# A half-precision Strassen matmul with GELU: staging, order and look-ahead changed

## The chip, the cores and the metric

The kernel runs on one NeuronCore of a Trainium2 chip. PE (TensorE) multiplies, DVE (VectorE) adds and transposes, ACT (ScalarE) copies, squares and applies GELU, POOL (GpSimd) issues loads and fetches, SP (SyncE) issues stores. The metric is the device time of one execution in microseconds (us).

## The reference, cut to what matters

```python
def reference(a: np.ndarray, b: np.ndarray) -> np.ndarray:   # 4096 x 4096, float32
    x = np.matmul(a, b)
    return 0.5 * x * (1 + np.tanh(np.sqrt(2 / np.pi) * (x + 0.044715 * x**3)))
```

## The kernel before, in words

**Tiling.** A, B and the output are cut into quadrants (11, 12, 21, 22) of 2048 x 2048. A block row `mb` (0 to 3) is 512 rows of each row half of A; a block column `nb` (0 to 3) is 512 columns of each column half of B. A group is a pair (mb, nb); there are 16, numbered 0 to 15, four to a block row. For each group the four output tiles of 512 x 512 are computed by Strassen's seven products M1 to M7 in float16: each product multiplies a sum or difference of A's quadrants (or one quadrant raw) by one of B's. The inner dimension of 2048 is handled in two chunks `c` of 1024, each in two quarters, so a product has four quarters `q`, and a quarter is 16 matmuls of 128 x 512: that is a step.

**Steps.** Everything is placed by a list of 504 steps, written as (group, product's place s, quarter q). Group 0 begins with 16 plain steps (chunk 0 without Strassen) and then has two steps for each product, numbers 16 to 29. Groups 1 to 9 have 28 steps each. In groups 10 to 15 the products M3 and M5, and in groups 13 to 15 also M2 and M1, are themselves split by Strassen into seven smaller products each, taken in the order of `PAIR`. `PRODUCTS` gives the order of products; a group before a change of block row uses `TURNING`, the last groups `FRESH`. The main loop at L1158 emits for each step: what stands in `before` for it (loads, transpositions, weighing), for the first six groups the operand sums of two steps later (`make_sums`), for later groups what the planner put into `tasks`, then `flush` and `combine` (pending output sums), and then the step's matmuls with `settle`, which takes finished sums from PSUM. [...]

**A.** A quadrant's part is loaded by POOL into a tile `stage` (two buffers, L192 and L221), as float16; DVE transposes it into `aT` (`turn_a`, L207); then ACT squares each row of the staged tile in place, with its sum (`weigh_row`, L267; `weigh_first` for the first block row, `weigh_rows` later), for a check of the magnitudes. Only then is the stage buffer free. In the first block row the text at L720 places loads (A.., B..), transpositions (T..) and weighing (W..) by step; names such as A22_1 give quadrant and chunk. Later block rows come in eight halves, in the order 11, 12, 22, 21; `TURNS` and `RAW_TURNS` give the step of each half's transposition as (s, q) counted from the group before the change, the load is placed `LOAD_AHEAD` steps before but not before the half two earlier is weighed, and the weighing takes the four steps after the transposition (L826 to L833).

**B.** Groups 0 to 5 load B raw into eight tiles `bR` whose places rotate between the quadrants when the block column changes (`b_slot`, L806 to L815): the next group's 12 takes the place of this group's 22. In the last of these groups for a block column, the operands of B that later groups will need are also stored to a scratch area in HBM: sums from `bS` by `make_sums` (L433) and raw quadrants by `keep_raw` (L402), both on SP's queue. `square` and `add_squares` (L300, L311) weigh B: ACT squares pieces, DVE adds them up; `TWO_GROUPS` places these for the block column that has two groups. Groups 6 to 15 fetch kept operands into tiles `bK` in the same eight places (`fetch`, L904), at most `FETCH_AHEAD` steps before use. `MAKES` lists when, in groups 6 to 10, operands for the later split products are made from kept ones by DVE (`make_split`, L997) and stored again (`k_split`); each entry is five sums in five consecutive steps.

**Sums of A.** From group 6 on the planner (L1104 to L1151) gives every operand sum of A a step: not earlier than a number of steps ahead of its use (`AHEAD` = 2, or `SPLIT_AHEAD` in split products), not before its buffer is free (three buffers `aS`, and in groups without makes three `bS` as well), and where an account of DVE's work per step leaves room (`sum_step`, L1041). Whole-block sums `aD` for the split products are planned by `plan_block` (L1075).

**Outputs.** `settle` (L621, for the last three groups `settle_fresh` at L665) copies PSUM tiles X and Y to `x7`, `x1` and `m5` tiles or combines them on DVE; `flush` and `emit` (L582, L608) apply GELU on ACT and store by SP. x7 has four buffers.

Of the kernel before, what the change touches and what calls it, by code (L numbers as in the profile page):

```python
# [16 lines left out]
P = 128  # L17
# [51 lines left out]
MAKES = (  # L69
    (6, 1, 0, 1, "M3"),  # L70
    (6, 2, 1, 1, "M5"),
    (6, 3, 2, 3, "M3"),
    (6, 4, 2, 3, "M5"),
    (7, 1, 3, 0, "M2"),
    (8, 2, 3, 2, "M3"),
    (8, 4, 0, 2, "M5"),
    (8, 5, 3, 2, "M1"),
    (9, 2, 0, 0, "M3"),
    (9, 2, 2, 0, "M5"),
    (9, 4, 2, 3, "M1"),  # L80
    (9, 5, 3, 3, "M2"),
    (10, 2, 2, 2, "M2"),
    (10, 4, 0, 0, "M1"),
)
STAY = ("M2", "M1")
STAY_AHEAD = 19
BLOCK_AHEAD = 12
SPLIT_AHEAD = 8
FETCH_AHEAD = 8
SPLITS = {M3_M5: (10, 11, 12, 13, 14, 15), M2_M1: (13, 14, 15)}  # L90
LOAD_AHEAD = 8

TURNS = ((2, 2), (3, 2), (4, 2), (5, 2), (6, 2), (7, 2), (9, 0), (10, 2))
RAW_TURNS = ((2, 2), (3, 2), (5, 2), (6, 1), (7, 1), (8, 1), (10, 1), (11, 1))

# [8 lines left out]

TWO_GROUPS = [x // 2 for x in range(16)] + [8 + 2 * x for x in range(16)]
N_WARM = 46
# [48 lines left out]
def half_path(  # L155
# [36 lines left out]
    def load_a(mb, quad, c, h=None):  # L192

        ih, kh = int(quad[0]) - 1, int(quad[1]) - 1
        n = NX if h is None else NX // 2
        x = 0 if h is None else h * n
        x0 = (ih * MH + mb * TM) // Q + x
        if not h:
            s = pool.tile([P, NX, RUN], F16, name="stage", tag="stage", bufs=2)
            staged[mb, quad, c] = s  # L200
        s = staged[mb, quad, c]
        return [
            (s[g * Q : (g + 1) * Q, x : x + n, :], a_v[kh, g, :, x0 : x0 + n, c * RUN : (c + 1) * RUN])
            for g in range(4)
        ]

    def turn_a(mb, quad, c, h=None):  # L207
# [5 lines left out]
        if mb:  # L213
            src = staged[mb, quad, h].rearrange("p x (c r) -> p c x r", c=CH)[:, c]
        else:
            src = staged[mb, quad, c][:, x, :]
        src = src.bitcast(U32).rearrange("p mb (jj q) -> p jj mb q", q=Q)
        dst = a_tiles[mb, quad, c].bitcast(U32).rearrange("p jj (mb q) -> p jj mb q", q=Q)
        nc.vector.transpose(dst[:, :, x, :], src)  # L219

# [65 lines left out]
    def weigh_first(quad, c, xs):  # L286

        ih, kh = int(quad[0]) - 1, int(quad[1]) - 1
        for x in xs:
            k = ((kh * CH + c) * 2 + ih) * NX + x  # L290
            weigh_row(stats["a"][:, k : k + 1], staged[0, quad, c][:, x, :])

# [372 lines left out]
    def settle_fresh(gi, name, i, X, Y):  # L665
# [6 lines left out]
        elif name == "M1":  # L672
            m1, x7 = keep("m5", X, 2), post["x7", i]
            tt(x7, x7, m1, ALU.add)
        elif name == "M4":
            emit(gi, i, 1, 0, new_y(), Y)
# [3 lines left out]
            waiting.append((gi, i, 0, 0, y, y))  # L680
        elif name == "M6":
            y = post.pop(("x1", i))
            tt(y, X, y, ALU.add)
            flush()
            waiting.append((gi, i, 1, 1, y, y))
# [34 lines left out]
    for n, whats in (  # L720
# [5 lines left out]
        (14, "T11_1 W11_1 A22_1 B11_1"),  # L726
        (16, "T12_1 W12_1:0-4"),
        (17, "W12_1:4-16 A21_1"),
        (18, "S2 S3 T22_1"),
        (23, "T21_1"),  # L730
        (34, "W22_1:0-1"),
        (35, "W22_1:1-2"),
        (36, "W22_1:2-3"),
        (37, "W22_1:3-4"),
        (38, "W22_1:4-5"),
        (39, "W22_1:5-6"),
        (40, "W22_1:6-7"),
        (41, "W22_1:7-8"),
        (42, "W22_1:8-9"),
        (43, "W22_1:9-10"),  # L740
        (44, "W22_1:10-11"),
        (45, "W22_1:11-12"),
        (46, "W22_1:12-13"),
        (47, "W22_1:13-14"),
        (48, "W22_1:14-15"),
        (49, "W22_1:15-16"),
        (50, "W21_1:0-1"),
# [73 lines left out]
    for gi in range(len(groups) - 1):  # L821
# [4 lines left out]
        for (quad, h), n in zip(halves, turns(gi)):  # L826
            at_step(max(n - LOAD_AHEAD, free_at.pop(0)), load, (load_half, (mb, quad, h)))
            free_at.append(n + 5)
            at_step(n, turn_half, mb, quad, h)
            for x in range(4):  # L830
                at_step(n + 1 + x, weigh_rows, mb, quad, h, list(range(NX // 2))[x * NX // 2 // 4 : (x + 1) * NX // 2 // 4])
            if h and quad in ("12", "21"):
                at_step(n + 5, weigh_half, mb, int(quad[0]) - 1)  # L833


    for nb, gi in last_raw.items():
        for s, (name, _, _, ob) in enumerate(PRODUCTS):
            for c in range(CH) if isinstance(ob, str) else ():
                at(gi, s, 2 * c, keep_raw, nb, name, ob, c)

# [263 lines left out]
    for gi in range(N_RAW, len(groups)):  # L1104
# [13 lines left out]
        for n in mine:  # L1118
# [14 lines left out]
            if not isinstance(o, str):  # L1133
                ahead = SPLIT_AHEAD if q in SPLIT else AHEAD
                only = any(n - ahead <= x <= n for x in makes) or makes and q not in SPLIT
# [17 lines left out]
    with tc.manual_schedule():  # L1153
# [4 lines left out]
        for n, step in enumerate(steps):  # L1158
            for fn, args in before.get(n, ()):
                fn(*args)  # L1160
            if n + AHEAD < len(steps):
                gi, s, q = steps[n + AHEAD]
                if s >= 0 and gi < N_RAW:
                    make_sums(gi, s, q)
# [9 lines left out]
            else:  # L1174
                multiply(*step)
            if step == (0, 2, QPH - 1):
                flush()
# [38 lines left out]
```

## Time and profile before

| what | us |
|---|---|
| median of 9 runs | 1571.2 |
| lowest and highest | 1567.64 and 1576.34 |
| profiled execution | 1575.39 |
| its span, first to last instruction | 1573.8 |
| PE busy | 1548.2 |
| DVE busy | 1139.0 |
| ACT busy | 601.3 |
| POOL busy (issuing) | 462.6 |
| end of the last matmul | 1567.5 |

The granted TensorE clock was 0.996 on average. In the lines shown below a timeline line has the start from the beginning of the span, the length, the engine, the line of the code, the operation, what it writes and reads, the shapes, the number of instructions merged, and in brackets the engine's idle time before it and what ended it. A line of the chain of waits has start, length and what was running. Line numbers are those of the kernel before.

### The profile page before, as it was taken

To read this page: it belongs to the slowest core of one execution; us is meant where nothing else is said; L and a number is where in the kernel's file an instruction comes from. 1 tells how busy PE (TensorE), PEld (TensorE's weight loads), DVE (VectorE), ACT (ScalarE), POOL (GpSimd) and SP (SyncE) were. 2 spreads that over 40 slices of the span, in tenths; PEclk is the share of its full clock that TensorE was granted. 3 is DMA by queue.
4 is the path that set the end of the run, shared out by engine and by line. 5 is a ranking of instruction groups with operands and counts; after the bars stand their busy time and mean duration, and the time that the engine had idled before them with its cause. 6 is when DMAs were issued, how large, how long until landed. Compare 5 with 4: busy or idle time off the path is not lost.

```text
span 1573.8 us, 22250 instructions
## 1 busy us (share of the span) xinstructions
PE 1548.2 (98%) x8110; PEld 794.5 (50%) x8110; DVE 1139.0 (72%) x1357; ACT 601.3 (38%) x1322; POOL 462.6 (29%) x830
## 2 busy tenths in 40 slices
PE   9999999999999999999999999999999999999998
PEld 4444444444444444444444444654746457677674
DVE  1597888889877887674656647978748677776774
ACT  5437456455543542111453211121345413232232
POOL 7763432441124311122231222221333312132130
PEclk9999999999999999999999999999999999999999
DMA  9999999994689988699997989897999959788693
GB/s 176 187 221 291 248 293 275 284 239 87 155 236 291 288 297 311 251 416 342 287 273 231 411 317 368 319 413 247 320 242 295 333 159 308 241 276 313 229 333 109
DMA packets 202789, 429.40 MB, mean 273 GB/s; under 512 B 20400, under 2 KB 102320, under 8 KB 200624
## 3 DMA queue, kind: packets, MB, share of 16 engines
q0 software_dynamic: 141472, 265.34, 65.5%
q1 hardware_dynamic: 61200, 162.56, 27.1%
q8 instruction: 66, 1.08, 0.3%
q14 instruction: 51, 0.42, 0.1%
HBM read 340.79 MB, written 162.53 MB: 320 GB/s over the span
## 4 chain that ended last, share of the span: by engine, by line
PE 74%; DMA 16%; DVE 4%; POOL 3%; issue 2%; ACT 1%; DVEq 0%; ACTq 0%; POOLq 0%
PE accX L466 35%; PE accY L466 26%; DMA stage<-in_a_dram 8%; PE accX L548 6%; PE accY L548 6%; DMA bR<-in_b_dram 4%; DMA k_split<-bS 2%; POOL bR L255 1%; POOL stage L255 1%; DMA k_M<-bS 1%; DVE aS L931 1%; DVE bS L428 1%; DVE x L619 1%; DVE bS L931 1%; DVE aT L219 0%
## 5 line engine op out<-in xcount | busy, mean ns | idle before, releaser
L466 PEld LDWEIGHTS <-aS 128*128 128x128 f16 x4192 | 410.1, 98 | 511.6 <-issue 13.8
L466 PE MATMUL accX<-bK,aS 128*128 128x512 f16 x1536 | 334.5, 379 | 2.4 <-DVE aS L931 2.1
L931 DVE TENSOR_TENSOR aS<-aT 128x2048 f16<-128x2048 f16 x182 | 216.6, 1217 | 90.6 <-PE accX L466 71.2
L466 PEld LDWEIGHTS <-aT 128*128 128x128 f16 x1600 | 156.6, 98 | 188.4 <-issue 0.4
L917 POOL DMA_DIRECT2D bK<-k_M x236 | 124.8, 533 | 398.2 <-PE accX L466 115.1
L255 POOL DMA_DIRECT2D bR<-in_b_dram x320 | 173.0, 543 | 213.1 <-DMA bR<-in_b_dram 105.4
L269 ACT ACTIVATE stage<-stage 128x512 f16<-128x512 f16 (+1 forms) x320 | 169.6, 532 | 140.3 <-DVE aT L219 101.4
L466 PE MATMUL accY<-bK,aS 128*128 128x512 f16 x896 | 195.0, 379 | 0.6 <-DVE aS L931 0.5
L610 ACT ACTIVATE x<-x 128x512 f32<-128x512 f32 x128 | 78.2, 628 | 251.5 <-DVE x L619 251.4
L466 PE MATMUL accX<-bS,aS 128*128 128x512 f16 x704 | 156.3, 383 | 6.9 <-DVE bS L428 4.3
L548 PEld LDWEIGHTS <-aS 128*128 128x128 f16 x1440 | 141.6, 98 | 26.4 <-DVE aS L931 3.4
L428 DVE TENSOR_TENSOR aS<-aT 128x2048 f16<-128x2048 f16 (+1 forms) x112 | 133.9, 1200 | 27.9 <-PE accX L466 16.6
L428 DVE TENSOR_TENSOR bS<-bR 128x2048 f16<-128x2048 f16 x110 | 133.4, 1216 | 25.0 <-PE accX L466 13.7
L309 ACT ACTIVATE square<-bR 128x1024 bf16<-128x1024 f16 x120 | 123.2, 1049 | 48.5 <-DVE energy L619 47.7
L255 POOL DMA_DIRECT2D stage<-in_a_dram x144 | 84.6, 592 | 190.5 <-ACT stage L269 129.3
L219 DVE STREAM_TRANSPOSE aT<-stage 128x1024 uint32<-128x1024 uint32 (+1 forms) x61 | 76.0, 1277 | 77.2 <-DMA stage<-in_a_dram 67.1
L577 ACT COPY x<-accX 128x512 f32<-128x512 f32 x116 | 67.7, 585 | 167.3 <-PE accX L466 154.3
L931 DVE TENSOR_TENSOR bS<-bK 128x2048 f16<-128x2048 f16 x70 | 84.1, 1218 | 25.3 <-DMA k_split<-bS 25.2
L619 DVE TENSOR_TENSOR x<-accY,x 128x512 f32<-128x512 f32 x116 | 77.2, 687 | 33.8 <-ACT y L610 23.9
L466 PE MATMUL accY<-bK,aT 128*128 128x512 f16 x448 | 97.8, 379 | 0.0
L466 PE MATMUL accX<-bK,aT 128*128 128x512 f16 x448 | 97.8, 379 | 0.0
L577 ACT COPY m<-accX 128x512 f32<-128x512 f32 x76 | 43.3, 581 | 124.1 <-PE accX L466 96.5
(70 smaller groups left out, 1518.6 us busy)
## 6 DMA issues: line engine op xcount, KB each, us to landing
bK<-k_M POOLq DMA_DIRECT2D x272, 512.0 KB, 10.0
bK<-k_split POOLq DMA_DIRECT2D x90, 512.0 KB, 6.6
bR<-in_b_dram POOLq DMA_DIRECT2D x320, 128.0 KB, 7.3
k_M<-bS SPq DMA_DIRECT2D x80, 512.0 KB, 6.5
k_split<-bS SPq DMA_DIRECT2D x70, 512.0 KB, 7.2
out_dram<-y SPq DMA_DIRECT2D x128, 256.0 KB, 6.5
out_dram<-x SPq DMA_DIRECT2D x128, 256.0 KB, 7.1
stage<-in_a_dram POOLq DMA_DIRECT2D x112, 256.0 KB, 8.7
```

The source lines that it names most:

```text
L219: nc.vector.transpose(dst[:, :, x, :], src)
L255: nc.gpsimd.dma_start(out=dst, in_=src)
L269: nc.scalar.activation(src, src, ACT.Square, accum_out=dst)
L309: nc.scalar.activation(t[:, :], src, ACT.Square)
L428: nc.vector.tensor_tensor(out=x, in0=y, in1=z, op=ALU.add if o[2] > 0 else ALU.subtract)
L466: nc.tensor.matmul(acc[:, :], sa[:, j // 2, i * P : (i + 1) * P, j % 2], sb[:, j, :], start=start and j == 0, stop=stop and j == 3, skip_g ...
L548: nc.tensor.matmul(banks[chain, i][:, :] if wide else out, sa[:, j // 2, r * P : (r + 1) * P, j % 2], sb[:, : NC] if wide else sb[:, j * N ...
L577: nc.scalar.copy(out=t[:, :], in_=src[:, :])
L610: nc.scalar.activation(y[:, :], src[:, :], ACT.Gelu_apprx_tanh)
L619: nc.vector.tensor_tensor(out=o[:, :], in0=x[:, :], in1=y[:, :], op=op)
L917: nc.gpsimd.dma_start(out=dst, in_=kept_unit(*key[1:])[:, x * w : (x + 1) * w])
L931: nc.vector.tensor_tensor(out=t, in0=y, in1=z, op=ALU.add if op > 0 else ALU.subtract)
```

## The change

- First group: the second chunk of A22 (`THIRD`) is staged in four x7 tiles instead of a stage buffer; its loads become 16 instead of 8, its two half transpositions four. It is weighed in steps 18 to 21, and A12's second chunk in steps 34 to 49, where A22's stood.
- First group: the operand sums for M6's last step are emitted after the matmuls and sums of step (0, 5, 3) instead of before (`C21_FIRST`).
- Group 1: M5's raw operand (B22) is stored two products later.
- Groups 3 and 4: `TWO_GROUPS` places B's squares earlier; the halves of A in the raw groups are weighed in two steps each instead of four, and `RAW_TURNS` moves four of the eight transpositions.
- Later groups: `MAKES` is arranged anew, sums may stand 5 steps ahead (`SUM_AHEAD`) instead of 2, those in split products 6 instead of 8, fetches and A's loads 9 instead of 8; `TURNS` moves A12's second half two steps earlier and A21's halves later.
- Last group: x1 is added to X in PSUM at M1 instead of to M6's result; M6's tiles go straight through GELU, the last one in two halves that two queues store.

```diff
 MAKES = (
-    (6, 1, 0, 1, "M3"),
+    (6, 0, 1, 0, "M3"),
+    (6, 1, 1, 1, "M3"),
     (6, 2, 1, 1, "M5"),
     (6, 3, 2, 3, "M3"),
-    (6, 4, 2, 3, "M5"),
-    (7, 1, 3, 0, "M2"),
+    (7, 0, 1, 2, "M1"),
+    (7, 5, 3, 0, "M2"),
     (8, 2, 3, 2, "M3"),
     (8, 4, 0, 2, "M5"),
-    (8, 5, 3, 2, "M1"),
-    (9, 2, 0, 0, "M3"),
-    (9, 2, 2, 0, "M5"),
-    (9, 4, 2, 3, "M1"),
+    (8, 5, 3, 0, "M5"),
+    (9, 1, 1, 2, "M2"),
+    (9, 2, 2, 3, "M5"),
+    (9, 4, 0, 3, "M1"),
     (9, 5, 3, 3, "M2"),
-    (10, 2, 2, 2, "M2"),
     (10, 4, 0, 0, "M1"),
 )
...
+SUM_AHEAD = 5
 BLOCK_AHEAD = 12
-SPLIT_AHEAD = 8
-FETCH_AHEAD = 8
+SPLIT_AHEAD = 6
+FETCH_AHEAD = 9
...
-LOAD_AHEAD = 8
+RAW_LOAD_AHEAD = 8
+WEIGH_STEPS = 2
+LOAD_AHEAD = 9
 
-TURNS = ((2, 2), (3, 2), (4, 2), (5, 2), (6, 2), (7, 2), (9, 0), (10, 2))
-RAW_TURNS = ((2, 2), (3, 2), (5, 2), (6, 1), (7, 1), (8, 1), (10, 1), (11, 1))
+TURNS = ((2, 2), (3, 2), (4, 2), (5, 0), (6, 2), (7, 2), (10, 1), (10, 3))
+RAW_TURNS = ((2, 3), (3, 3), (5, 2), (6, 1), (7, 1), (8, 1), (11, 0), (11, 0))
...
-TWO_GROUPS = [x // 2 for x in range(16)] + [8 + 2 * x for x in range(16)]
+TWO_GROUPS = (0, 0, 1, 1, 2, 2, 3, 3, 4, 4, 4, 4, 5, 5, 5, 5, 5, 7, 10, 12, 14, 16, 18, 18, 20, 20, 24, 26, 27, 27, 28, 29)
+C21_FIRST = (0, 5, QPH - 1)
+THIRD = ("22", 1)
...
+        if (quad, c) == THIRD:
+            tiles = staged[mb, quad, c] = staged.get((mb, quad, c), [])
+            ts = []
+            for i in range(x // (NX // RT), (x + n) // (NX // RT)):
+                t = pool.tile([P, NC], F32, name="x7", tag="x7", bufs=RT).bitcast(F16)
...
+        elif (quad, c) == THIRD:
+            n = NX // RT
+            parts = [
+                (slice(i * n, (i + 1) * n), staged[mb, quad, c][i]) for i in range(x.start // n, x.stop // n)
+            ]
...
+            if gi == len(groups) - 1:
+                x1 = post.pop(("x1", i))
+                tt(X, X, x1, ALU.add)
...
-        elif name == "M6":
+        elif gi == len(groups) - 1:
+            flush()
+            if i < RT - 1:
+                emit(gi, i, 1, 1, new_y(), X)
+                return
+            mb, nb = groups[gi]
+            r0, c0, w = MH + mb * TM + i * P, NH + nb * NC, NC // 2
+            for x, queue in enumerate((nc.sync, nc.scalar)):
+                y = new_y()
+                nc.scalar.activation(y[:, :w], X[:, x * w : (x + 1) * w], ACT.Gelu_apprx_tanh)
+                queue.dma_start(out=out[r0 : r0 + P, c0 + x * w : c0 + (x + 1) * w], in_=y[:, :w])
+        else:
...
-        (16, "T12_1 W12_1:0-4"),
-        (17, "W12_1:4-16 A21_1"),
-        (18, "S2 S3 T22_1"),
+        (16, "T12_1"),
+        (17, "A21_1"),
+        (18, "S2 S3 T22_1 W22_1:0-4"),
+        (19, "W22_1:4-8"),
+        (20, "W22_1:8-12"),
+        (21, "W22_1:12-16"),
         (23, "T21_1"),
-        (34, "W22_1:0-1"),
...
+        (34, "W12_1:0-1"),
...
-            at_step(max(n - LOAD_AHEAD, free_at.pop(0)), load, (load_half, (mb, quad, h)))
-            free_at.append(n + 5)
+            at_step(max(n - (LOAD_AHEAD if gi >= N_RAW else RAW_LOAD_AHEAD), free_at.pop(0)), load, (load_half, (mb, quad, h)))
+            slow = WEIGH_STEPS if gi < N_RAW else 4
+            free_at.append(n + slow + 1)
...
-                at(gi, s, 2 * c, keep_raw, nb, name, ob, c)
+                at(gi, s + 2 * (gi == 1 and name == "M5"), 2 * c, keep_raw, nb, name, ob, c)
...
-                ahead = SPLIT_AHEAD if q in SPLIT else AHEAD
+                ahead = SPLIT_AHEAD if q in SPLIT else SUM_AHEAD
...
-                if s >= 0 and gi < N_RAW:
+                if s >= 0 and gi < N_RAW and step != C21_FIRST:
                     make_sums(gi, s, q)
...
+            if step == C21_FIRST:
+                make_sums(*steps[n + AHEAD])
```

## The prediction

> **What bounds the kernel now.** I read the page's first part, then who PE (TensorE) waited for, then PE's timeline around each wait, then the chain of waits behind the longest one, and last DVE's (VectorE's) timeline where DVE itself waited.
>
> ```profile
> PE 1548.2 (98%) x8110; PEld 794.5 (50%) x8110; DVE 1139.0 (72%) x1357; ACT 601.3 (38%) x1322; POOL 462.6 (29%) x830
> ```
>
> PE is busy for nearly all of the span, and its 128x512 matmuls start 0.216 us apart (a step of 16 takes 3.45 us). The change removes none of the 8110 matmuls, so it can win only PE's waits, PE's slow stretches and the tail. The waits in total, by what PE waited for (us in total, times, longest):
>
> ```profile
> PE accX L466 <- DVE bS L428: 4.5, 2, 4.3
> PE accX L548 <- DVE aS L931: 3.1, 1, 3.1
> PE accX L466 <- DVE aS L428: 2.4, 2, 1.7
> PE accX L466 <- DVE aS L931: 2.1, 3, 1.3
> PE accX L466 <- ACT m L577: 1.9, 2, 1.5
> PE accY L466 <- DVE x L619: 1.8, 1, 1.8
> PE accY L497 <- DMA bR<-in_b_dram: 1.1, 1, 1.1
> ```
>
> With two smaller rows (0.5 and 0.3) that is 17.7 us. The timeline of PE says where (start, length, idle before in brackets):
>
> ```profile
> 84.99 1.47 PE L466 MATMUL accX<-bS,aS 128*128 128x512 f16 x6 [0.71 <-DVE aS L428]
> ...
> 114.69 7.07 PE L466 MATMUL accY<-bS,aS 128*128 128x512 f16 x32 [1.77 <-DVE x L619]
> ...
> 160.61 9.64 PE L466 MATMUL accX<-bS,aS 128*128 128x512 f16 x32 [4.32 <-DVE bS L428]
> ...
> 444.76 3.63 PE L466 MATMUL accX<-bR,aS 128*128 128x512 f16 x16 [1.69 <-DVE aS L428]
> ...
> 451.63 4.62 PE L466 MATMUL accX<-bS,aS 128*128 128x512 f16 x20 [1.52 <-ACT m L577]
> ...
> 961.25 2.98 PE L466 MATMUL accX<-bK,aS 128*128 128x512 f16 x13 [1.33 <-DVE aS L931]
> ...
> 1203.10 5.55 PE L548 MATMUL accX<-bK,aS 128*128 128x512 f16 x32 [3.14 <-DVE aS L931]
> ```
>
> Two waits cost more than their idle time. The 32 matmuls at 160.61 take 9.64 us where 32 take 7.07 elsewhere (line 114.69): 2.6 us more. The two sub-steps at 1203.10 take 5.39 us to the next one where the same pair takes 3.70 at 1105.85: 1.7 more. All waits and slow stretches: 17.7 + 2.6 + 1.7 = 22.0 us.
>
> The chain behind the longest wait is a stream of loads of B:
>
> ```profile
> 118.49 7.60 DMA bR<-in_b_dram
> ...
> 126.37 13.04 DMA bR<-in_b_dram
> ...
> 139.69 13.07 DMA bR<-in_b_dram
> ...
> 153.04 6.29 DMA bR<-in_b_dram
> 159.33 0.01 issue
> 159.34 1.24 DVE bS L428
> ```
>
> A piece takes 7.6 us, then 13, then 6.3: in between something else uses the DMA engines. And at the two changes of A's row block DVE stands at a transposition until A lands:
>
> ```profile
> 440.62 2.37 DVE L219 STREAM_TRANSPOSE aT<-stage 128x1024 uint32<-128x1024 uint32 x2 [7.35 <-DMA stage<-in_a_dram]
> ...
> 1174.29 2.37 DVE L219 STREAM_TRANSPOSE aT<-stage 128x1024 uint32<-128x1024 uint32 x2 [3.73 <-DMA stage<-in_a_dram]
> ...
> 1190.02 2.37 DVE L219 STREAM_TRANSPOSE aT<-stage 128x1024 uint32<-128x1024 uint32 x2 [4.19 <-DMA stage<-in_a_dram]
> ```
>
> [...] after the 4.32 us wait eleven matmuls start 0.43 us apart. [...] work behind a waiting transposition waits too, as at 440.62. [...] the shortest store at the end took 2.0.
>
> **The change part by part.**
>
> *A22's second part in x7's tiles.* POOL stood 3.26 us (70.0 to 73.27) until ACT had weighed A11's buffer. That wait goes. Eight issues become sixteen half-size ones: at 0.54 to 0.59 us (the bR and stage rows) +4.6 us of POOL, so A22's issues end near 79.1 (before 77.8), its last piece lands near 82 (before 82.84), and B11's eight pieces, issued 1.3 us later into an emptied queue, land some 1.0 us earlier, near 87. Two transpositions become four: at most 4 x 0.71 (the 128x512 row) for 2 x 1.22, +0.4 of DVE. W22's 16 rows (0.40 each on ACT, 6.4 us) move to steps 18 to 21, ahead of x7's copies; W12's take their place later, one a step. At steps 16 to 19 ACT has 8 rows instead of 16 ahead of M5's copies. Of 0.71 + 0.40 at M7's opening I take 0.6; between -0.5 (ACT's rows late for M7's copies) and 1.1.
>
> *C21's sums first.* At 109.4 to 114.0 DVE makes four operands (4 x 1.22) and only then M2's subtractions from accY, for which M6 waits 1.77. With the last two operands behind them, the four subtractions (2.5 us) end near 114.2 and the two operands near 116.5, while M6's second step would start at 112.8 + 3.45 = 116.2. Gain 1.77 - 0.3 = 1.5; between 0.5 and 1.8.
>
> *M5's raw B22 kept two products later (group 1).* Two stores of 1 MB (k_M<-bR, issued 130.16 and 132.16, landed 144.85 and 147.98, each 3.1 to 3.2 us after the store before it) leave the stream in front of B21's second half, which landed at 159.12. With 1.0 from above that is 159.1 - 6.3 - 1.0 = 151.8; bS 1.24 later. PE, 2.1 us earlier by the two parts above, wants it at 156.1 - 2.1 = 154.0, so about 0 is left; I keep 0.5. Of 4.32 + 2.6 = 6.9 the gain is 6.4; bounds -1 (none of the stores' time comes back, see B) and 6.9. What is late next: the stores now stand at steps 42 and 44, and group 2's B12, which takes B22's place, must wait for them on POOL: about 6 us, with B22 queued behind. Before, those land at 199 to 209 and are summed from 218 on: 9 us of cover. If that were gone each us would be one of PE's.
>
> *Two steps of weighing, squares earlier (groups 3 to 4).* A12's first half is turned at step 108, weighed in four steps until 411.64, and only then A22's load leaves (411.93); the next leaves at 423.64 and lands at 440.50, where DVE waits 7.35. Weighing in two steps frees each buffer about 6 us earlier, so the second A22 half lands near 430 to 434, before its turn's time of about 433. The energy sums (0.68 each) in steps 116 to 124 move ahead of step 115. The cover for up to four squares (1.05 each) in a step is ACT's idle half. A21's halves now turn together at step 130, 4.9 us of DVE with 5.4 us of M1's sums behind; by 133 DVE has done the same total as before, so the 0.3 us wait there stays. Gain 1.69 + 1.52 = 3.2; bounds 1.5 and 3.5.
>
> *The makes of split operands.* Two runs of five started two steps apart in group 9; their stores (7 to 9 us to land) held the three bS buffers. They are now spread over groups 6 to 10, nearly always one a step. The waits at 951 to 961 (0.37 + 0.39 + 1.33) and at 754 (0.48) are 2.6; I take 2.4, bounds 0 and 2.6.
>
> *Sums up to five steps ahead, A12's second half turned two steps earlier, loads and fetches one step earlier.* In group 11 that half lands at 1174.17, since its load stands behind fetches; its turn now stands at step 342 (1166.7). So DVE waits there, with M1's eight sums (1164.95 to 1170.56) behind: 1174.2 + 2.4 + 5.6 = 1182.2. M2 needs accY from 1180.5 to 1183.1, bank by bank: just enough. In exchange M5's blocks are added from step 343 on, not after 1190. Of 3.14 + 1.7 = 4.8 I take 3.3; bounds -3 (each us that A lands later) and 4.8.
>
> *The end.* M6's last tile: DVE 0.70, ACT 0.63, store 3.54 from its issue become two gelus of half width (between 0.37, the 128x256 copy, and 0.60) and two stores of half size on two queues, 2.0 to 3.5 us. Gain 0.7 to 2.2; I take 1.2. The added X + x1 (4 x 0.68) lies under M4's 13.8 us.
>
> Sum: 0.6 + 1.5 + 6.4 + 3.2 + 2.4 + 3.3 + 1.2 = 18.6. For new small waits of DVE's changed order I take off 1.5 (two like the 0.5 to 0.7 us ones now there). 17.1 us of the profiled 1575.39 (span 1573.8) gives 1558.3; the median of the nine runs, 1571.2, lies 4.2 below that execution: 1554.1.
>
> **The rivals.** B, the stream of B stays late: M6's outputs and sums come 2 us earlier and take the place of the stores. Then B21 lands at 158.1 and is summed at 159.3, PE waits from 154.0 on, 5.3 us and again 2.6 of slow clock: 7.9 for the 6.9 of before. 17.1 - 6.4 - 1.0 = 9.7, so 1561.5. [...] against, these are the same bytes, only the 2 MB are gone. C, the early turn holds DVE in group 11: A lands 5 us later against PE than now, PE loses these and the 3.3: 17.1 - 8.3 = 8.8, so 1562.4. For it, A's pieces take 12 to 16 us there. D, slower: [...] fetches go one step further ahead and wait for PE to free their place (POOL bK for PE accX: 169.0 us in 27 waits), and A's halves stand behind them. Each half late by a step costs 3.45 us; from five of the 16 halves of the two later turns on (17.1 / 3.45) the gain is gone, with eight the time is 1571.2 - 17.1 + 27.6 = 1582. Against it: in group 7 all halves landed before DVE asked. E, no change: the summary speaks of B11 ahead of A22, which no line of the diff does; if most else balances out, 1571.
>
> **How the numbers follow.** Within 0.2% (3 us) is what cannot be told from no change. The forecast has 0.62, B 0.12, C 0.14, better than all 0.02, E 0.03, D 0.07: faster 0.90, same 0.03, slower 0.07. The floor is 22.0 - 1.1 (the first load's wait is untouched) + 2.2 = 23.1 less: 1548. The range ends beyond B and C at 1565.
>
> **What would show it.** Right: no bracket over 1 us at M6 of group 0, at group 1's M7, in group 4's M5 and M7 and in group 9; no half-speed stretch after 160; the last store about 4 us after the last matmul. Wrong: DVE waiting at L219 longer than before near group 11's end with PE waiting behind it, or POOL's stage pieces landing after their turns.

## The result, and the profile after

The changed kernel takes 1560.1 us (median of 10 runs, 1555.24 to 1564.05), the kernel before 1571.2 in the same comparison. The ratio is 0.9922, with a 95% interval of 0.9907 to 0.9937: 12 us faster, give or take 2. The predicted 1554.1 is 6.0 us too low; the sign and the range of 1548 to 1565 hold.

The profiled execution of the changed kernel took 1558.97 us (span 1557.4) where that of the kernel before took 1575.39 (span 1573.8). These two differ by 16.4 us, the medians only by some 11. That gap matters below. The page's first part:

```profile
PE 1544.6 (99%) x8110; PEld 794.5 (51%) x8110; DVE 1139.6 (73%) x1359; ACT 600.9 (39%) x1323; POOL 463.8 (30%) x830
```

The work is the same, 8110 matmuls; PE is busy 3.6 us less, most of it the slow stretch of 2.6 us in group 1 that went (granted clock 0.50 from 159.04 to 165.86). Who PE waited for, in total, times and longest:

```profile
PE accX L575 <- DVE x L646: 2.2, 1, 2.2
PE accX L493 <- DVE bS L455: 1.7, 1, 1.7
...
PE accY L524 <- ACT c L540: 0.7, 1, 0.7
PE accY L493 <- DVE x L646: 0.6, 1, 0.6
PE accY L493 <- DVE bS L455: 0.4, 1, 0.4
```

Without the first 1.4 us of the program, where PE waits for a table in both kernels, 5.6 us are left of 17.7. PE's timeline at the places that the prediction showed (M7's opening and M6 in group 0, then two new places, group 2's M7 and group 12's first split products):

```profile
83.98 14.04 PE L493 MATMUL accX<-bS,aS 128*128 128x512 f16 x64
...
112.41 3.61 PE L493 MATMUL accY<-bS,aS 128*128 128x512 f16 x16 [0.58 <-DVE x L646]
116.47 3.61 PE L493 MATMUL accY<-bS,aS 128*128 128x512 f16 x16 [0.45 <-DVE bS L455]
...
253.03 7.28 PE L493 MATMUL accX<-bS,aS 128*128 128x512 f16 x33 [1.71 <-DVE bS L455]
...
1187.70 5.54 PE L575 MATMUL accX<-bK,aS 128*128 128x512 f16 x32 [2.16 <-DVE x L646]
```

The brackets of 4.32 us (group 1), 1.69 and 1.52 (group 4) and 1.33 (group 9) have no counterpart: PE runs through those places. Group 0's M6 still waits, twice. The line at 253.03 is new. The line at 1187.70 stands where 1203.10 stood before, with 2.16 us idle for 3.14, and now waits for DVE's reads of PSUM instead of an operand. Its 32 matmuls take 5.54 us, 1.7 more than the 3.88 that the same 32 took in the second profile of the kernel before; the granted clock was 0.53 from 1187.70 to 1190.00.

DVE's timeline shows what stands behind that last wait:

```profile
1158.37 2.37 DVE L244 STREAM_TRANSPOSE aT<-stage 128x1024 uint32<-128x1024 uint32 x2 [10.84 <-DMA stage<-in_a_dram]
...
1179.99 2.36 DVE L244 STREAM_TRANSPOSE aT<-stage 128x1024 uint32<-128x1024 uint32 x2
1182.28 1.18 DVE L976 TENSOR_TENSOR aS<-aD 128x2048 f16<-128x2048 f16 x1
1183.38 2.47 DVE L646 TENSOR_TENSOR x<-x,accY 128x512 f32<-128x512 f32 x4
1185.78 2.47 DVE L646 TENSOR_TENSOR x<-accY,x 128x512 f32<-128x512 f32 x4
```

DVE waits 10.84 us for A12's second half, and M1's sums, emitted behind that transposition, start after it, at 1160.67. Then DVE works without a break until it reads M2's blocks, which ends at 1188.2. PE needs that place and starts at 1187.70, 0.5 us before the last read ends.

One profile is one execution. To see which waits belong to the program I compared the start of every one of the 504 steps in all 14 profiles of this study. A column is the time, in us, by which its steps take longer than each of them takes in the profile where it is quickest; the span is 1547.7 us plus the row's sum. "Rest" is below 0.15 everywhere.

| profile | before step 16 | g0 M5 to M7 | g0 M6 | g1 M7 | g2 M7 | g4 | g6-9 makes | g11-12 | tail | span |
|---|---|---|---|---|---|---|---|---|---|---|
| before | 1.3 | 1.4 | 1.9 | 7.1 | 0 | 4.0 | 3.6 | 5.5 | 1.2 | 1573.8 |
| before, again | 0.9 | 1.2 | 1.9 | 6.1 | 0 | 4.4 | 4.6 | 0.3 | 0.8 | 1568.2 |
| raw store alone | 0.6 | 4.1 | 0.8 | 0 | 0 | 4.2 | 6.5 | 0.3 | 0.7 | 1565.1 |
| changed | 1.6 | 0.1 | 1.4 | 0 | 1.9 | 0 | 0 | 4.0 | 0.6 | 1557.4 |
| changed, again | 1.4 | 1.1 | 1.8 | 0 | 0 | 0 | 0 | 0.4 | 0 | 1552.6 |
| raw store back | 1.2 | 0.9 | 1.3 | 8.8 | 0 | 0 | 0 | 0 | 0.4 | 1560.6 |
| raw stores at 40, 41 | 0.7 | 0.6 | 1.8 | 0 | 0 | 0 | 0 | 1.4 | 1.0 | 1553.3 |
| turn at (5, 2) | 1.5 | 1.9 | 0.8 | 0 | 0 | 0 | 0 | 0 | 1.0 | 1553.1 |
| weighing in four steps | 0.6 | 1.6 | 1.8 | 0 | 0.5 | 1.6 | 0 | 1.6 | 0.9 | 1556.6 |
| C21's sums before | 1.6 | 0.4 | 4.7 | 0 | 0 | 0 | 0 | 4.4 | 0.7 | 1559.5 |
| makes of before | 2.6 | 0.4 | 1.8 | 0 | 1.2 | 0 | 8.8 | 1.6 | 0.4 | 1564.7 |
| stores and turn | 1.4 | 1.1 | 1.7 | 1.1 | 0 | 0 | 0 | 8.5 | 0.4 | 1562.0 |
| A22 in a stage buffer | 1.0 | 1.4 | 0.3 | 0 | 0 | 0 | 0 | 0.7 | 0.3 | 1551.5 |
| put together | 1.0 | 0.9 | 0.3 | 0 | 0 | 0 | 0 | 4.7 | 0.5 | 1555.2 |

Some columns are the program's own (group 1, group 4, the makes): they stand in every profile with the code in question, and in no other but for 1.1 us at group 1 in "stores and turn", where B21's second chunk landed at 155.2, before the raw stores were issued at 160.2. Groups 11 to 12, and in part group 0's M7 and group 2, change from one execution of the same kernel to the next.

### The profile page after: what moved, and what is told of

Its sections match the earlier page's. It is cut to its first block, busy times and chain, and to the rows that moved or that the text cites. A ratio compares the mean times of both kernels' runs of the same rounds, so it can differ in the third digit from the quotient of the medians.

```text
span 1557.4 us, 22302 instructions
## 1 busy us (share of the span) xinstructions
PE 1544.6 (99%) x8110; PEld 794.5 (51%) x8110; DVE 1139.6 (73%) x1359; ACT 600.9 (39%) x1323; POOL 463.8 (30%) x830
## 5 line engine op out<-in xcount | busy, mean ns | idle before, releaser
L962 POOL DMA_DIRECT2D bK<-k_M x228 | 121.0, 535 | 415.8 <-PE accX L493 117.2
L294 ACT ACTIVATE stage<-stage 128x512 f16<-128x512 f16 (+1 forms) x304 | 163.0, 538 | 105.9 <-DVE aT L244 67.3
L493 PE MATMUL accX<-bS,aS 128*128 128x512 f16 x704 | 153.1, 379 | 1.7 <-DVE bS L455 1.7
L280 POOL DMA_DIRECT2D stage<-in_a_dram x136 | 80.1, 595 | 139.1 <-ACT stage L294 105.7
```

Of the source, the lines that this page charges most:

```text
L280: nc.gpsimd.dma_start(out=dst, in_=src)
L294: nc.scalar.activation(src, src, ACT.Square, accum_out=dst)
L493: nc.tensor.matmul(acc[:, :], sa[:, j // 2, i * P : (i + 1) * P, j % 2], sb[:, j, :], start=start and j == 0, stop=stop and j == 3, skip_g ...
L962: nc.gpsimd.dma_start(out=dst, in_=kept_unit(*key[1:])[:, x * w : (x + 1) * w])
```

## The experiments

All ratios are to the kernel before, each with its 95% interval.

### Both kernels again

No edit.

> The changed kernel unaltered, profiled a second time. The first profile showed 5.6 us of waits of PE, the longest the 2.2 us for M2's sums of group 11 (1185.8 to 1188.2) and 1.9 us at the second chunk of M7 in group 2. If these are the program's own, they stand at the same steps and within 0.5 us of the same lengths, and the time is 1560 us. If they are chance of one execution (how the DMA traffic fell), at least one of the two is gone or sits at another step, and the medians can't be explained by them.

Measured: 1558.8 us, 0.9925 (0.9912 to 0.9939). The second profile has neither the wait at group 2 (1.9 to 0) nor, but for 0.4 us, that at group 12. They are chance of an execution, as the second branch of the expectation has it.

> The kernel before unaltered, profiled a second time. Theory: the waits at M7 of group 1 (7.1 us with the slow clock) and in group 4 (4.0) are the program's own and stand again within 0.5 us; the wait ahead of group 12's split products (5.3 us in the first profile, 0.3 in a run with the first part of the kernel changed alone) follows the landing of A and may be anything between 0 and 5.5. Rival: the first profile's waits of group 12 are the rule, 4 us or more again.

Measured: 1569.7 us. Group 1 has 6.1, group 4 has 4.4; group 12's 5.5 us is now 0.3. PE's timeline there, without a bracket:

```profile
1199.89 3.88 PE L548 MATMUL accX<-bK,aS 128*128 128x512 f16 x32
```

So the first profile of the kernel before held 5.2 us that its other executions need not have.

### M5's raw store in group 1

Put back in the changed kernel:

```diff
-                at(gi, s + 2 * (gi == 1 and name == "M5"), 2 * c, keep_raw, nb, name, ob, c)
+                at(gi, s, 2 * c, keep_raw, nb, name, ob, c)
```

> The changed kernel with M5's raw B22 of group 1 stored where it was before. Theory: the later store alone removed the wait at M7 of group 1 (7.1 us between the two profiles) and alone caused the new one at M7 of group 2 (1.9 us); so the first is back with 6 to 7 us, the second is gone, and the time is 5.2 us longer, 1565.3 us. Rival 1: the wait at group 2 comes from something else in the new order of group 2; then it stays and the time is 7 us longer, 1567. Rival 2: it was the earlier B11 and A22 of the first group that brought B21 forward; then nothing comes back, 1560.

Measured: 1565.0 us, 0.9967 (0.9956 to 0.9978), against 0.9925 for the changed kernel on the same chip: 6.6 us lost, for 5.2 expected. PE's timeline of this kernel:

```profile
148.02 7.07 PE L493 MATMUL accX<-bS,aS 128*128 128x512 f16 x32
161.40 18.89 PE L493 MATMUL accX<-bS,aS 128*128 128x512 f16 x76 [6.32 <-DVE bS L455]
```

The wait is back, 6.32 us and 2.3 more in the matmuls behind it (76 take 18.89 us, where 0.216 us apart they would take 16.6), longer than before because PE arrives 1.2 us earlier and B21's sum comes 0.8 us later (160.13 for 159.34). Group 2's wait is absent, which says little, since the changed kernel can be without it too.

The same edit alone in the kernel before:

```diff
-                at(gi, s, 2 * c, keep_raw, nb, name, ob, c)
+                at(gi, s + 2 * (gi == 1 and name == "M5"), 2 * c, keep_raw, nb, name, ob, c)
```

> The kernel before with one part of the change alone: M5's raw B22 of group 1 stored two products later. Theory: the stream of B21 ends 6.3 us earlier, at about 152.8; PE wants the operand at 156.1, so the wait of 4.3 us and the 2.6 us of slow clock after it go, and at M7 of group 2 one of about 2 us comes: 5 us less, 1566.2 us. Rival (B of the prediction): other traffic takes the place of the stores, B21 stays late: 1571.

Measured: 1565.5 us, 0.9967 (0.9957 to 0.9978): 5.2 us gained, as expected. PE's timeline:

```profile
139.71 10.52 PE L466 MATMUL accX<-bR,aS 128*128 128x512 f16 x48
150.07 27.79 PE L466 MATMUL accX<-bS,aS 128*128 128x512 f16 x128
```

128 matmuls without a bracket: the wait is gone. B21's second chunk, which landed at 159.1 before, landed at 150.9 here, and at 151.6 and 152.2 in the two profiles of the changed kernel, where the prediction had worked out 151.8; so no other traffic took the place of the stores. Rival B falls. No wait came at group 2 in this execution. From both sides the store is worth 5 to 7 us, half of the whole change.

Between the two places, one step apart:

```diff
-                at(gi, s + 2 * (gi == 1 and name == "M5"), 2 * c, keep_raw, nb, name, ob, c)
+                at(gi, s + (gi == 1 and name == "M5"), 2 + c if gi == 1 and name == "M5" else 2 * c, keep_raw, nb, name, ob, c)
```

> The changed kernel with the two raw stores of group 1 at steps 40 and 41 instead of 42 and 44, so after B21's second chunk has landed, but earlier for group 2. Theory: POOL, which stood 17.7 us until the first store landed at 169.5, goes on 5 to 7 us earlier, the stream of B for group 2 ends 2 us or more earlier, and the wait of 1.9 us at M7 of group 2 is gone while that at M7 of group 1 stays away: 1558.2 us. Rival 1: POOL is then held by the next buffer in the row (M1's and M4's operands), the stream ends as late as now: 1560. Rival 2: the stores meet the end of B21's stream and the wait at M7 of group 1 is partly back, 1 to 4 us: 1561 to 1564.

Measured: 1558.6 us, 0.9922 (0.9908 to 0.9936), no difference to the changed kernel that this measurement can tell. POOL's timeline in the changed kernel, and after it in this one:

```profile
170.10 4.30 POOL L280 DMA_DIRECT2D bR<-in_b_dram  x8 [17.69 <-DMA k_M<-bR]
```

```profile
166.72 3.75 POOL L280 DMA_DIRECT2D bR<-in_b_dram  x7 [13.71 <-DVE energy L646]
```

The store no longer holds POOL, DVE's energy sums do; so POOL goes on 3.4 us earlier, not 5 to 7, a part of rival 1. Group 2's wait is not there, but it was not there in the second profile of the changed kernel either, so this one profile doesn't prove the remedy. In all, three of the eight profiles with the stores at 42 and 44 have that wait (0.5, 1.2 and 1.9 us), none of the three with stores at 40 and 41 and none of the three with the stores where they were.

### The change of row block in groups 11 and 12

A12's second half turned two steps later:

```diff
-TURNS = ((2, 2), (3, 2), (4, 2), (5, 0), (6, 2), (7, 2), (10, 1), (10, 3))
+TURNS = ((2, 2), (3, 2), (4, 2), (5, 2), (6, 2), (7, 2), (10, 1), (10, 3))
```

> The changed kernel with A12's second half turned at (5, 2) again, as before, instead of (5, 0). Theory: the eight sums of M1 no longer stand behind the transposition that waits for A; they run in DVE's idle 10.8 us, the sums of A ahead of group 12 start 5 us earlier, M2's blocks are read as soon as PE has them, and of the 3.8 us still lost around the first split products of group 12 at least 3 go: 1556 to 1557 us. Rival 1: DVE's total between the landing at 1158 and the end of M5 is the bound, so nothing is won: 1560. Rival 2: the half's buffer comes free two steps later and A22's second half lands late in its turn; the old wait at M7 of group 12 (3.1 and 1.7 us before) is back: 1561 to 1565.

Measured: 1556.9 us, 0.9914 (0.99 to 0.9928); the intervals overlap with the changed kernel's, so the gain of 2 us is not shown by times. DVE's timeline:

```profile
1157.62 2.37 DVE L244 STREAM_TRANSPOSE aT<-stage 128x1024 uint32<-128x1024 uint32 x2
...
1170.25 2.36 DVE L244 STREAM_TRANSPOSE aT<-stage 128x1024 uint32<-128x1024 uint32 x2
...
1176.83 0.69 DVE L646 TENSOR_TENSOR x<-x,accY 128x512 f32<-128x512 f32 x1 [0.55 <-PE accY L493]
```

A landed at 1156.91, so that a turn at (5, 0) could have started 5.4 us after M4's first step (1151.60), which by the table below costs 1.7 us. Here DVE has done M1's sums ahead of it, A22's first half is turned at 1170.25, and DVE waits for PE at M2's blocks instead of PE for DVE: 0 lost. With the turn at (5, 0) the loss follows the landing. The eight profiles that have it, ordered by how long after the start of M4's first step (step 342) the transposition could start:

| profile | start after step 342 | PE waits | lost in the matmuls after it |
|---|---|---|---|
| raw store back | 0.8 | 0 | 0 |
| changed, again | 4.2 | 0.4 | 0 |
| A22 in a stage buffer | 4.4 | 0.6 | 0 |
| raw stores at 40, 41 | 5.1 | 1.3 | 0 |
| makes of before | 5.3 | 1.6 | 0 |
| weighing in four steps | 5.4 | 1.6 | 0 |
| changed | 6.1 | 2.3 | 1.7 |
| C21's sums before | 6.4 | 2.7 | 1.7 |

From 3.75 us on, each us later is one us of PE's: 6.07 - 3.75 = 2.32. This is rival C's mechanism at the place that it named.

The later turn and the two stores at 40 and 41 together (both diffs above):

> The changed kernel with the raw stores of group 1 at steps 40 and 41 and A12's second half turned at (5, 2). Theory: neither the wait at M7 of group 2 nor that ahead of group 12's split products is there, whatever the DMA traffic of an execution does; against the changed kernel that is 0 to 1.9 and 0 to 4.5 us by its profiles, 2 us in the middle: 1557 us, with waits of PE under 5 us in all. Rival: the two together change nothing that can be measured, 1559 to 1560, because the executions with these waits are rare.

Measured: 1555.8 us, 0.9899 (0.9879 to 0.992), the lowest ratio of the study, with an interval that overlaps the changed kernel's. Its profile, though, caught an execution in which A landed late, and refutes "whatever the DMA traffic of an execution does". DVE's timeline:

```profile
1181.76 2.37 DVE L244 STREAM_TRANSPOSE aT<-stage 128x1024 uint32<-128x1024 uint32 x2 [6.50 <-DMA stage<-in_a_dram]
...
1187.71 2.48 DVE L646 TENSOR_TENSOR x<-x,accY 128x512 f32<-128x512 f32 x4
1190.10 2.48 DVE L646 TENSOR_TENSOR x<-accY,x 128x512 f32<-128x512 f32 x4
```

A12's second half started 10.2 us after M4's first step, and the next transposition, of A22's first half, had M2's reads behind it: 5.2 us of waiting and 8.5 lost in all. Moving one transposition makes another the first to be late.

So in the last run both stand behind M2's reads, with the raw stores at 40 and 41 and A22's second chunk of group 0 in a stage buffer again (see the next part):

```diff
-TURNS = ((2, 2), (3, 2), (4, 2), (5, 2), (6, 2), (7, 2), (10, 1), (10, 3))
+TURNS = ((2, 2), (3, 2), (4, 2), (5, 2), (7, 1), (7, 2), (10, 1), (10, 3))
```

> Put together from what the runs before showed: the changed kernel with A22's second chunk of group 0 in a stage buffer again, the raw stores of group 1 at steps 40 and 41, A12's second half turned at (5, 2), and A22's first half turned at (7, 1), so that DVE reads M2's blocks from PSUM ahead of it. Theory: PE's wait ahead of group 12's split products is set by transpositions that wait for A with M2's reads behind them; with none of them ahead of those reads the wait is at most 0.5 us, however late A lands, group 0 ends as early as with the stage buffer, and the time is 1553 to 1555 us. Rival 1: the operand sums behind the two transpositions of A22, now closer together, come late, and the wait moves to M7 of group 12 or into group 8, 1 to 4 us: 1556 to 1558. Rival 2: the wait of group 12 has another cause, the late blocks of the split products' own sums, and stays between 0 and 7 us: 1556.

Measured: 1560.2 us, 0.9921 (0.99 to 0.9943), nothing gained over the changed kernel. The wait ahead of the split products is 0, as the theory has it, and others of 4.6 us in sum stand five to nine steps later, a case of rival 1. DVE's timeline and PE's:

```profile
1190.41 2.37 DVE L244 STREAM_TRANSPOSE aT<-stage 128x1024 uint32<-128x1024 uint32 x2 [4.99 <-DMA stage<-in_a_dram]
...
1193.81 1.66 DVE L589 TENSOR_TENSOR join<-accX,join 128x256 f32<-128x256 f32 x4
```

```profile
1194.74 1.91 PE L575 MATMUL accX<-bK,aS 128*128 128x256 f16 x16 [0.69 <-DVE join L589]
1199.18 1.03 PE L575 MATMUL accY<-bK,aS 128*128 128x256 f16 x8 [2.54 <-DVE accY L589]
```

A22's second half lands at 1190, and now the split products' own sums stand behind its transposition. The order on DVE chooses who waits; the lateness is that of A's transfers. Why they take longer in one execution than in the next was not settled.

### A22's second chunk and C21's sums in group 0

A22's second chunk in a stage buffer again, with the weighing (`THIRD` and the rows of L765 to L790 as before):

```diff
-THIRD = ("22", 1)
+THIRD = ("", 0)
...
-        (16, "T12_1"),
-        (17, "A21_1"),
-        (18, "S2 S3 T22_1 W22_1:0-4"),
...
+        (16, "T12_1 W12_1:0-4"),
+        (17, "W12_1:4-16 A21_1"),
+        (18, "S2 S3 T22_1"),
```

> The changed kernel with the second chunk of A22 in group 0 staged and weighed as before (a stage buffer instead of four x7 tiles). Theory: POOL stands again 3.3 us for A11's buffer, A22 and B11 land later, and the wait at M7's opening in group 0 is again 1.4 us or more, where the changed kernel has 0.1 to 1.3: 0.6 us longer, 1560 us. Rival 1: that wait reaches 4 us with the slow clock, as it did with the raw store alone changed: 1562 us. Rival 2: the stage was never what M7 waited for: 1559.

Measured: 1553.9 us, 0.9906 (0.9884 to 0.9929). The interval overlaps the changed kernel's, so a gain from taking the part out is not shown by the times; that the part is worth nothing, or less, is to be seen in the steps. POOL's timeline of the changed kernel, then of this one:

```profile
72.42 7.78 POOL L280 DMA_DIRECT2D x<-in_a_dram  x14 [0.99 <-DMA stage<-in_a_dram]
80.19 4.29 POOL L280 DMA_DIRECT2D bR<-in_b_dram  x8
```

```profile
72.47 4.56 POOL L280 DMA_DIRECT2D stage<-in_a_dram  x8 [3.28 <-ACT stage L294]
77.02 1.09 POOL L280 DMA_DIRECT2D bR<-in_b_dram  x2
```

Without the x7 tiles POOL stands 3.28 us and is nevertheless 3.2 us earlier at B11, since it issues 8 transfers in place of 16. B11 landed from 84.2 to 88.9 in the changed kernel (84.6 to 90.2 in its second profile), from 83.1 to 87.7 here. DVE then, in the changed kernel and in this one:

```profile
86.96 1.22 DVE L455 TENSOR_TENSOR aS<-aT 128x2048 f16<-128x2048 f16 x1
89.17 1.22 DVE L455 TENSOR_TENSOR bS<-bR 128x2048 f16<-128x2048 f16 x1 [1.00 <-DMA bR<-in_b_dram]
```

```profile
87.69 1.21 DVE L455 TENSOR_TENSOR aS<-aT 128x2048 f16<-128x2048 f16 x1
88.82 1.22 DVE L455 TENSOR_TENSOR bS<-bR 128x2048 f16<-128x2048 f16 x1
```

From this sum on DVE is busy without a break until M6. M7's opening loses 0.9 us on average in the nine profiles with x7 tiles, 1.4 here; what that wins is lost at M6 (1.4 and 1.8 in the two profiles of the changed kernel, 0.3 here and in the last run). Both places together lose 1.7 us here and 1.2 in the last run, and 1.5 to 3.4, 2.5 on average, in the eight profiles with the tiles and C21's new order. Group 1 starts at 119.6 us here and at 119.9 and 121.2 in the changed kernel.

C21's sums emitted ahead of M2's again:

```diff
-                if s >= 0 and gi < N_RAW and step != C21_FIRST:
+                if s >= 0 and gi < N_RAW:
                     make_sums(gi, s, q)
...
-            if step == C21_FIRST:
-                make_sums(*steps[n + AHEAD])
```

> The changed kernel with the operand sums for M6's last step of group 0 emitted ahead of M2's sums again. Theory: the wait at M6's start returns to about 1.8 us and the 0.6 us at its second step goes: 0.6 us longer, 1560.7 us, to be seen in the steps and hardly in the median. Rival: the prediction's size, 1.5 us longer, 1561.6. Second rival: with the earlier start of group 0 there is no wait at either place, 1560.

Measured: 1562.7 us, 0.9946 (0.9929 to 0.9962), some 3 us slower than the changed kernel, more than any of the three answers said, though the ends of the intervals still overlap. The steps bear it out: M6 loses 4.7 us for 1.4 and 1.8. PE's timeline:

```profile
115.10 8.58 PE L493 MATMUL accY<-bS,aS 128*128 128x512 f16 x32 [3.00 <-DVE x L646]
```

3.00 us idle, and 1.5 of slow clock (granted 0.50 from 115.10 to 117.20). M2's sums, for which M6 waits, in DVE's timeline of this kernel and then of the changed one:

```profile
114.36 2.48 DVE L646 TENSOR_TENSOR x<-x,accY 128x512 f32<-128x512 f32 x4
```

```profile
111.68 2.47 DVE L646 TENSOR_TENSOR x<-x,accY 128x512 f32<-128x512 f32 x4
```

From B11's sum DVE needs 24.8 us without a break to reach them in the old order (89.58 to 114.36 here, 89.18 to 113.96 in the kernel before) and 22.5 in the new one (89.17 to 111.68; 88.82 to 111.33 with the stage buffer). So C21's order gains with and without the tiles: M6 loses 4.7 us against 1.4 and 1.8 with them, and 1.9 (both profiles of the kernel before) against 0.3 (both profiles with the new order and a stage buffer) without. The x7 tiles make B11, and with it DVE, late, and C21's order takes that back.

### Weighing in groups 3 and 4

```diff
-WEIGH_STEPS = 2
+WEIGH_STEPS = 4
```

> The changed kernel with the halves of A in the raw groups weighed in four steps again; squares and turns stay as changed. Theory: the shorter weighing frees the stage buffers and brings A22's second half ahead of its turn; with four steps DVE waits at that transposition again, and the two waits of group 4 are back with at least 2 of their 3.7 us: 1562 to 1564 us. Rival: the earlier squares of B and the moved turns did it, and nothing comes back: 1560.

Measured: 1557.8 us, 0.9923 (0.9899 to 0.9947), no difference in the time. DVE's wait for A22's second half is back in full (7.88 us here, 7.35 before), but in the steps only 1.6 us of PE's time, of 4.0 and 4.4 in the kernel before. DVE's timeline, then PE's:

```profile
432.53 2.37 DVE L244 STREAM_TRANSPOSE aT<-stage 128x1024 uint32<-128x1024 uint32 x2 [7.88 <-DMA stage<-in_a_dram]
```

```profile
436.07 3.63 PE L493 MATMUL accX<-bR,aS 128*128 128x512 f16 x16 [0.23 <-DVE aS L455]
439.53 1.89 PE L493 MATMUL accX<-bS,aS 128*128 128x512 f16 x8
442.34 7.86 PE L493 MATMUL accX<-bS,aS 128*128 128x512 f16 x35 [0.92 <-ACT m L604]
```

Less than the 2 us expected: the weighing is the smaller part, the rest lies with the squares of B and the moved turns, which were not taken apart.

### The list of makes

`MAKES` as before, all else as changed (the diff is that of the change the other way round, here its last part):

```diff
-    (9, 1, 1, 2, "M2"),
-    (9, 2, 2, 3, "M5"),
-    (9, 4, 0, 3, "M1"),
+    (9, 2, 0, 0, "M3"),
+    (9, 2, 2, 0, "M5"),
+    (9, 4, 2, 3, "M1"),
     (9, 5, 3, 3, "M2"),
+    (10, 2, 2, 2, "M2"),
     (10, 4, 0, 0, "M1"),
```

> The changed kernel with the list of makes of before. Theory: the crowded makes caused the waits around 754 and 951 to 961 us; they come back with 2.4 to 3.5 us: 1562.5 to 1563.6 us. Rival: sums five steps ahead and fetches nine ahead are what removed them, and at most 0.5 us comes back: 1560.

Measured: 1561.1 us, 0.9937 (0.9918 to 0.9955), 2 us more than the changed kernel by the ratios, with intervals that overlap. Its profile has 8.8 us there, more than either profile of the kernel before (3.6 and 4.6). DVE's timeline, then PE's:

```profile
936.35 1.22 DVE L976 TENSOR_TENSOR bS<-bK 128x2048 f16<-128x2048 f16 x1 [4.20 <-DMA k_split<-bS]
...
948.69 1.23 DVE L976 TENSOR_TENSOR bS<-bK 128x2048 f16<-128x2048 f16 x1 [4.32 <-DMA k_split<-bS]
949.83 1.22 DVE L976 TENSOR_TENSOR aS<-aT 128x2048 f16<-128x2048 f16 x1
```

```profile
951.11 8.77 PE L493 MATMUL accX<-bK,aS 128*128 128x512 f16 x32 [4.68 <-DVE aS L976]
```

DVE waits for the store of an earlier make to free its buffer, and PE's operand (DVE's last line) stands behind. The rival, that the sums five steps ahead had removed these waits, falls. Whether the new list alone, without the sums five steps ahead, would do was not tried; nor was any of the other look-aheads, or the new end of the last group, changed alone.

## Why the prediction was right or wrong

**The step that failed: from the profiled execution to the median.** The sum took the profiled 1575.39 to 1558.3; the changed kernel's profiled execution took 1558.97. Then I subtracted 4.2, since before's median lay that much below its profile. But after's median lies 1.1 above its own. That is 4.2 + 1.1 = 5.3 of the miss of 6.0. The reason for the 4.2 stands in the table: of the 5.5 us that before's first profile lost at groups 11 to 12, its second lost 0.3, and that execution took 1569.7 where the median of its comparison was 1569.9. I counted 3.3 of them as removed and then the same surplus once more as the distance to the median. The 1.1 stays open. The spans of the two profiles of each kernel (1573.8 and 1568.2, 1557.4 and 1552.6) are on average 16 us apart, about what the terms below sum to, and the medians only 11 to 12. So in the other executions the changed kernel must lose some 4 us more, set against the kernel before, than these four profiles show; where was not seen. The agreement of the two profiled times is itself partly luck, as the terms show.

| term | predicted gain | lost before, two profiles | lost after, two profiles | reading |
|---|---|---|---|---|
| A22 in x7 tiles (M7's opening) | 0.6 | 1.4, 1.2 | 0.1, 1.1 | 0.5 over the nine profiles, given back at M6 |
| C21's sums first (M6) | 1.5 | 1.9, 1.9 | 1.4, 1.8 | 0.3; 1.6 without the x7 tiles |
| M5's raw store | 6.4 | 7.1, 6.1 | 0, 0 | 6.6, less 0 to 1.9 at group 2 |
| weighing, squares, turns of group 4 | 3.2 | 4.0, 4.4 | 0, 0 | 4.2 |
| makes | 2.4 | 3.6, 4.6 | 0, 0 | 4.1 |
| groups 11 and 12 | 3.3 | 5.5, 0.3 | 4.0, 0.4 | 0.7, mostly chance |
| tail | 1.2 | 1.2, 0.8 | 0.6, 0 | 0.3 over all profiles |

**A22 and C21** together were to give 2.1 us and gave about 1. The step that failed is "B11's eight pieces land some 1.0 us earlier, near 87": they landed 0.7 to 2.1 us later than before (83.5 to 88.1), as the 16 half-size issues took POOL until 80.2 where I had worked out 79.1, so that B11 was issued 2.4 us later and not 1.3, and B11 is what DVE then waits for. The gain at M7's opening was right in size. C21's order was right in mechanism and in size: without the tiles M6 loses 0.3 us for 1.9. With the tiles, whose delay makes the old order cost more, it is worth some 3.

**M5's raw store**: right in mechanism and size. "What is late next" was half right: POOL stands behind the store, 17.7 us in all. But what was late was not group 2's B12 or B22, with 9 us of cover, but the end of the stream, B21's second chunk, where the cover was about used up: 1.9 us in one profile of the changed kernel, 0 in the other.

**Group 4**: right, at the upper end, and group 4's small wait that I took to stay went too. I gave most of it to the weighing; that holds for 1.6 us.

**The makes**: right in cause; 2.4 was under-sized because I took the waits of one profile, where executions lose 3.6 to 6.5 us.

**Groups 11 and 12**: the working of DVE's order was right (8.0 us from A's landing at 1174.2 to the end of M1's sums at 1182.2; it was 1158.25 to 1166.2), but "just enough" left out the sums of A queued between M1's sums and M2's reads, 17 us of DVE without a break. "I take 3.3" against a wait that this profile alone had was the wrong kind of term: it is a wait of chance, in both kernels, and should have gone into the range. One of the prediction's own signs of being wrong was there in the changed kernel's first profile: DVE stood 10.84 us at the transposition where it had stood 3.73, with PE waiting behind it, and a stretch at a granted clock of 0.50 followed (1187.86 to 1191.27).

**The tail**: two gelus of 0.38 us replaced sum and gelu, but the two half stores took 3.93 and 3.34 us to land (3.31 and 2.72 in the second profile) for 3.54 before. From the second of the last four on, the full stores land 0.6 us behind each other in both kernels (1571.23, 1571.86 and 1572.48 in the kernel before), and the two halves 0.3 (1555.74 and 1556.05, after the last full one at 1555.42 in the changed one): the halves landed closer behind each other, but only after the full stores issued ahead of them. The low end of my range, 2.0 us, was that of a store issued after the one ahead of it had landed (1566.35 to 1568.36 in the kernel before, the store ahead at 1558.79).

**The 1.5 taken off** for new small waits was about met: 1.9 us at group 2 in one profile, 0 in the other.

**The rivals.** B fell with the raw store alone; D was seen only in small: in group 7 one of A's halves is now late, DVE waits 3.9 us for it in the changed kernel's first profile and 6.0 in the second, and PE never waits for that; E fell. C's mechanism is real, one us for one us (0.4 us of waiting at 4.2 after M4's first step, 2.7 at 6.4), but A didn't land later than before, so its price was within what the kernel lost before as well (7.5 us after M4's first step in the first profile of the kernel before, 6.0 in that of the changed one).

**A version that beats both?** The raw stores at 40 and 41 with the later turn (0.9899), and A22 in a stage buffer (0.9906), have the lowest ratios, but neither is separated from the changed kernel's 0.9922 and 0.9925 by its interval, and the kernel put together from their parts (0.9921) bears no gain out.

## What to carry to other kernels

Before a wait seen in one profile is counted as a gain, ask whether it waits for a transfer: here such a wait was 5.5 us in one execution and 0.3 in the next, and if the profiled time lies above the median, that distance may be the very wait that was just counted. A transposition that waits for a load, put ahead of reads of PSUM on the same engine, made PE pay one us for each us of the load's lateness once the slack of 3.75 us was gone; moving it handed the lateness to whatever stood behind it next. Cutting a load into halves to fill other buffers doubled what POOL had to issue (16 transfers for 8, until 80.2 us for 77.0), and here the load behind it was the one that got late.

## What the runs showed of the hardware that was not expected

PE fell to half clock after shorter idle times than the 4.32 and 3.14 us in the prediction. The windows view of the changed kernel behind the wait of 2.16 us, with busy times and counts by engine and then the granted clock:

```profile
1187.70:1190.00 2.30, 2.30 (x10) 1.43 (x10) 2.14 (x4) 2.30 (x6) 0.00 (x0) 0.53 1.01 365
```

The clock is 0.53 here: it was 0.50 from 1187.86 to 1191.27 and 1.00 before and after, and 1.7 us are lost by it. A wait of 3.00 us with C21's sums before had 0.50 behind it (115.10 to 117.20), and the kernel with the raw store alone lost 4.1 us around a wait of 2.2 at M7's opening of group 0. Behind a wait of 2.54 us at 1199.18 in the last run the clock stayed at 1.00 (1199.10 to 1204.00). The second profile of the kernel before has both cases, the shorter wait with slower matmuls behind it and the longer without:

```profile
443.46 5.31 PE L466 MATMUL accX<-bR,aS 128*128 128x512 f16 x16 [1.98 <-DVE aS L428]
...
957.90 4.28 PE L466 MATMUL accX<-bK,aS 128*128 128x512 f16 x19 [3.51 <-DVE aS L931]
```

After 1.98 us idle 16 matmuls take 5.31 us, where 3.6 is usual; after 3.51 us idle 19 take 4.28, 0.216 us apart as at full clock. So the wait of 1.98 us cost 3.7 in all and that of 3.51 only itself: the length of the wait alone didn't decide it.

The first profiles of the two kernels have three stretches at a granted clock of 0.50 between the first matmul and the last: 159.04 to 165.86 and 1203.52 to 1206.93 before, 1187.86 to 1191.27 in the changed kernel. In the 3.41 us ahead of each PE was busy for 0.66, 0.42 and 1.25 us. Over the waits of 1.69 and 1.52 us in group 4 before, PE was busy for 1.72 us (442.32 to 445.73) and 1.89 (449.14 to 452.55), and the clock was 1.00 there and in the 3.41 us behind each. What decides whether half clock follows was not shown.
